# Seven products in place of eight for 37 more weight units of a streaming-encoder block

## The chip, the cores and the metric

The kernel runs on one core of a Trainium2 chip, in one launch. The metric is device time in microseconds (us) of one execution; lower is better. TensorE (PE) does matrix products into PSUM, VectorE (DVE) and ScalarE (ACT) do elementwise work, GpSimd (POOL) a little, and SyncE (SP) issues the weight transfers. Each engine runs its own instructions strictly in the order of the program, and engines wait for each other through semaphores.

## The reference

One layer of an encoder block over 256 rows of 2048 columns, all in float32:

```python
x = x + 0.5 * swiglu(rms_norm(x, ffn1_norm), ffn1_w_gate, ffn1_w_up, ffn1_w_down)
h = rms_norm(x, mix_norm)
proj = h @ w_in          # then four pooling groups and four gated-linear-attention heads
x = x + concat([y_pool, y_gla]) @ w_out
x = x + mem_cross_attention(rms_norm(x, xattn_norm), rms_norm(mem, mem_norm), w_q, w_kv, w_o)
x = x + 0.5 * swiglu(rms_norm(x, ffn2_norm), ffn2_w_gate, ffn2_w_up, ffn2_w_down)
out = rms_norm(x, final_norm)
# swiglu(h, wg, wu, wd) = (silu(h @ wg) * (h @ wu)) @ wd, with 5632 hidden columns
```

## The kernel before, in words

**Units.** The weights are streamed in units of 1 MB: a tile `raw` of 128 x 2048, three of them in flight. A float32 product is made of three products of a faster type: each factor is split into a high part (a rounded copy) and a low part (the rest), and high x high, high x low and low x high are added in PSUM. So for each unit ScalarE makes `wh` from `raw` (line 218), VectorE makes `wl = raw - wh` (line 219), and PE does 24 matmuls with 512 moving columns (`products`). `wh` and `wl` have three buffers each. The activations are held transposed and split in the same way in `xs` (what is normed from x) and `ys` (hidden rows, mixer or attention output), as 16 column groups k of 128 columns by 256 rows.

**The stream.** `Stream` (lines 34 to 90) is a list of units with other work between them: `st.op(f, n)` puts work n units later, and a unit is prepared two units ahead of its use. The order of instructions on each engine is then fixed at build time by a scheduler that plays the program through; on the chip nothing is reordered.

**Plain blocks.** `block_t` (line 293) takes eight units, four column quarters of two k-groups each, into two PSUM tiles of 128 x 2 x 512, and hands each tile to an evict function. PSUM holds four such tiles.

**Seven-product blocks.** `block_s` (line 393) takes a pair of k-groups as a 2 x 2 block product in the Strassen-Winograd form: seven products in place of eight, so 21 matmuls in place of 24. For this, sums of the weight quarters are made on VectorE in a tile `T` (lines 347 to 351, one buffer) and split into `wh` and `wl`, while the raw quarters are split into `xh` and `xl` (two buffers, 128 x 1536); the sums of activations come from `part_sums`, in a tile `xe`. Only the units 0, 2 and 4 of a block (`PAIRS`) are made in this way; the other five are plain. A block holds all four PSUM tiles: two with parts (P1, P6, P7, P5) and two with whole results. `combine` (lines 426 to 435) adds the parts up in a tile `sg`, one ScalarE copy and three VectorE adds; `join` (line 437) adds them to the whole results.

**Feed-forward.** `ffn` (line 649) goes through the hidden columns in three parts of 4, 4 and 3 groups of 512 (`FF_PARTS`). In each part come gate and up blocks by twos, an odd last column that has gate and up side by side (`wtwo`), and then the down product of the part. Gate blocks get a Silu (`ev_gate`, line 663), up blocks a product with it (`ev_up`, line 668). `turn` (line 673) transposes a finished group of hidden rows on PE into a PSUM tile `ph` and splits it into `ys`. The down product, the mixer's output product (`w_out`) and attention's (`w_o`) are written by `into_x` (line 617): two blocks, each of which adds two tiles to x (`residual`, line 595) and, where a norm follows, transposes the new x on PE and splits it into `xs` (`fold`, lines 602 to 615, with the scaled split of lines 210 and 211).

**What is seven and what is plain.** Seven-product blocks are all gate and up blocks by twos but the very first gate block of each feed-forward: 18 blocks, 54 units. Plain are those two, the odd columns, all down products, `w_out` and `w_o`. The mixer's input, q, and k/v products are made by `block_a` and `block_b` in a form of their own. The second feed-forward's last down product has a form of its own too (`down_end`).

Of the kernel before, what the change touches and what calls it, by code (L numbers as in the profile page):

```python
# [14 lines left out]
P = 128  # L15
# [77 lines left out]
def build(ctx, tc, I, out):  # L93
# [231 lines left out]
    def part_sums(act, ext, i, g):  # L325

        t = scope["pool"].tile([P, 4 * NB], F32, tag="T", name=uid("T"))
        a = t[:, :NB].rearrange("p (k s) -> p k s", k=2)
        e = t[:, NB : 2 * NB].rearrange("p (n s) -> p n s", n=4)
        nc.vector.tensor_tensor(  # L330
            out=a, in0=f32(act[:, 2 * g : 2 * g + 2, 0, :]), in1=f32(act[:, 2 * g : 2 * g + 2, 1, :]),
            op=ALU.add,
        )
        a11, a21, a12, a22 = (a[:, k, h * P : (h + 1) * P] for k in range(2) for h in range(2))
        nc.vector.tensor_tensor(out=e[:, 3], in0=a11, in1=a21, op=ALU.subtract)
        nc.vector.tensor_tensor(out=e[:, 1], in0=a22, in1=a21, op=ALU.subtract)
        nc.vector.scalar_tensor_tensor(
            out=e[:, 2], in0=e[:, 1], scalar=-1.0, in1=a11, op0=ALU.mult, op1=ALU.subtract
        )
        nc.vector.tensor_tensor(out=e[:, 0], in0=a12, in1=e[:, 2], op=ALU.add)  # L340
        split(ext[:, i, 0], ext[:, i, 1], e)
# [30 lines left out]
    def seven(banks, act, ext, i, g, first, later, weights):  # L372
# [3 lines left out]
        n4, n1, s2, s3 = ([ext[:, i, p, n] for p in range(2)] for n in range(4))  # L376
# [6 lines left out]
        order = ("P1", "P7", "P5", "P6", "P2", "P3", "P4") if first else (  # L383
            "P1", "P2", "P3", "P7", "P5", "P6", "P4")
        for n in order:
            (a, b), wh, wl = table[n]
            for j, (x, w) in enumerate(((a, wh), (a, wl), (b, wh))):
                nc.tensor.matmul(  # L388
                    banks[n], x, w, start=first and j == 0,
                    stop=not later and n in ("P1", "P5", "P6", "P7") and j == 2,  # L390
                )

    def block_s(srcs, act, ext, pairs, evict, delays=(0, 0)):

        held, n = {}, len(srcs)

        def open_banks():
            a, b, c, d = (ptile(uid("pt")) for _ in range(4))
            held["ps"] = (d, c)
            held["parts"] = (a, b)  # L400
            held["banks"] = {
                "P1": a[:, 0], "P6": a[:, 1], "P7": b[:, 0], "P5": b[:, 1],
                "P2": c[:, 0], "P4": c[:, 1], "P3": d[:, 0],
            }

        def unit_s(g):
            def fn(weights):
                if g == pairs[0]:
                    open_banks()
                seven(held["banks"], act, ext, pairs.index(g), g, g == pairs[0], g != pairs[-1],  # L410
                      weights)
            return fn

        def unit_p(g):
            def fn(wh, wl):
                wh, wl = (w.rearrange("p (k j n) -> p k j n", j=2, n=NB) for w in (wh, wl))
                for j in (1, 0):
                    for h in range(2):
                        for kk in range(2):

                            fresh = (j, h) == (0, 1) and g == min(set(range(n)) - set(pairs)) and kk == 0
                            products(held["ps"][j][:, h, :], act, 2 * g + kk, h, wh[:, kk, j],
                                     wl[:, kk, j], fresh, g == n - 1 and kk == 1)
            return fn

        def combine():
# [8 lines left out]
            nc.vector.tensor_tensor(out=e[:, 3], in0=b[:, 1], in1=e[:, 1], op=ALU.add)  # L435

        def join(j):
# [859 lines left out]
```

## Time and profile before

| what | value |
|---|---|
| median of 3 runs | 2137.7 us (2137.11 to 2137.98) |
| profiled execution | 2138.64 us |
| its span, first to last instruction | 2136.9 us |
| mean granted TensorE clock | 0.998 |
| TensorE busy | 2115.0 us, 99% |
| VectorE busy | 1425.8 us, 67% |
| ScalarE busy | 1006.0 us, 47% |

A row of the groups names line, engine, operation, the tiles written and read, the shape and the count, then the busy time and the mean length of one in ns, then the idle time of the engine just before them and what ended it. A row of the windows names a stretch and the busy time of each engine in it. A row of the chain of work that ended last has its start, its length and the line.

### The profile page before, as it was taken

How to read it: one execution, taken by the hardware profiler on the slowest of the kernel's cores; microseconds unless marked ns; L12 is line 12 of the kernel's file. 1: busy time of each engine (PE TensorE's matmuls, PEld its weight loads, DVE VectorE, ACT ScalarE, POOL GpSimd, SP SyncE). 2: the span in 40 equal slices, each digit the busy share in tenths (PEclk: the TensorE clock that was granted, in tenths of full speed). 3: DMA queues.
4: the chain of work that ended last, by engine and by line, in shares of the span. 5: the costliest groups of instructions: out<-in, count | busy, mean ns of one | idle time of the engine just before them, and what ended most of it. 6: DMA issues, size and time to landing. Idle time of an engine off the chain costs nothing.

```text
span 2136.9 us, 24071 instructions
## 1 busy us (share of the span) xinstructions
PE 2115.0 (99%) x10032; PEld 1769.1 (83%) x10032; DVE 1425.8 (67%) x1189; ACT 1006.0 (47%) x890; POOL 14.2 (1%) x41
## 2 busy tenths in 40 slices
PE   9999999999999999999999999999999999999998
PEld 7888887888888888888888888888888887888886
DVE  8786588856765576565666454567874788658744
ACT  7454354534444545455445443455443445434433
POOL 0000000000000000000000000000000000000001
PEclk9999999999999999999999999999999999999999
DMA  7556665666656655557655555666566655766663
GB/s 277 197 197 237 217 214 177 207 230 216 215 197 238 216 161 181 172 173 281 220 189 162 168 168 173 196 202 207 186 236 217 204 200 189 244 210 213 236 217 118
DMA packets 143317, 435.92 MB, mean 204 GB/s; under 512 B 9828, under 2 KB 13000, under 8 KB 142824
## 3 DMA queue, kind: packets, MB, share of 16 engines
q1 hardware_dynamic: 143176, 434.38, 60.1%
q8 instruction: 78, 1.28, 0.2%
q14 instruction: 31, 0.25, 0.0%
q10 hardware_dynamic: 32, 0.01, 0.0%
HBM read 417.58 MB, written 16.78 MB: 203 GB/s over the span
## 4 chain that ended last, share of the span: by engine, by line
PE 97%; DVE 2%; ACT 1%; issue 0%; DMA 0%; SPq 0%; DVEq 0%; ACTq 0%
PE pt L291 58%; PE pa L276 15%; PE pt L388 12%; PE pb L291 6%; PE pe L291 3%; ACT wh L218 1%; PE ph L678 1%; DVE wl L219 1%; PE pl L1071 1%; PE pv L1106 1%; PE px L608 0%; DMA x<-in_x 0%; PE px L562 0%; PE po L941 0%; DVE sg L439 0%
## 5 line engine op out<-in xcount | busy, mean ns | idle before, releaser
L219 DVE TENSOR_TENSOR wl<-raw,wh 128x2048 fp32r<-128x2048 f32 (+2 forms) x328 | 739.8, 2258 | 515.5 <-ACT wh L218 515.1
L218 ACT CAST wh<-raw 128x2048 fp32r<-128x2048 f32 (+2 forms) x329 | 618.4, 1881 | 626.3 <-PE pt L291 415.4
L291 PE MATMUL pt<-wh,xs 128*128 128x512 f32 x1952 | 620.1, 390 | 1.7 <-ACT wh L218 1.7
L291 PE MATMUL pt<-wh,ys 128*128 128x512 f32 x1728 | 534.5, 389 | 0.0
L291 PEld LDWEIGHTS pt<-wh,xs 128*128 128x128 f32 x1952 | 366.4, 188 | 78.1 <-ACT wh L218 2.5
L291 PE MATMUL pt<-wl,xs 128*128 128x512 f32 x976 | 380.4, 390 | 0.0
L291 PEld LDWEIGHTS pt<-wh,ys 128*128 128x128 f32 x1728 | 324.1, 188 | 66.8
L291 PE MATMUL pt<-wl,ys 128*128 128x512 f32 x864 | 336.3, 389 | 0.0
L276 PE MATMUL pa<-xs,wh 128*128 128x512 f32 x896 | 318.6, 399 | 2.1 <-DVE t L250 1.7
L276 PE MATMUL pa<-xs,wl 128*128 128x256 f32 x896 | 249.4, 281 | 0.0
L291 PEld LDWEIGHTS pt<-wl,xs 128*128 128x128 f32 x976 | 183.5, 188 | 37.9
L276 PEld LDWEIGHTS pa<-xs,wh 128*128 128x128 f32 x896 | 168.4, 189 | 41.6 <-issue 2.0
L291 PEld LDWEIGHTS pt<-wl,ys 128*128 128x128 f32 x864 | 162.2, 188 | 33.6
L218 ACT CAST wh<-T 128x2048 fp32r<-128x2048 f32 x54 | 103.1, 1909 | 171.1 <-DVE T L351 162.7
L219 DVE TENSOR_TENSOR wl<-T,wh 128x2048 fp32r<-128x2048 f32 x54 | 123.8, 2293 | 86.4 <-ACT wh L218 86.0
L276 PEld LDWEIGHTS pa<-xs,wl 128*128 128x128 f32 x896 | 169.9, 190 | 1.6 <-issue 0.2
L218 ACT CAST xh<-raw 128x1536 fp32r<-128x1536 f32 x54 | 80.1, 1483 | 98.6 <-DMA raw<-in_ffn_w_gate 36.6
L291 PE MATMUL pb<-wh,xs 128*128 128x512 f32 x384 | 121.7, 392 | 0.5 <-DVE ys L211 0.5
L388 PE MATMUL pt<-wh,xe 128*128 128x512 f32 x324 | 109.5, 390 | 0.8 <-DVE ys L219 0.7
L219 DVE TENSOR_TENSOR xl<-raw,xh 128x1536 fp32r<-128x1536 f32 x54 | 94.8, 1755 | 15.8 <-ACT xh L218 15.5
L291 PEld LDWEIGHTS pb<-wh,xs 128*128 128x128 f32 x384 | 72.1, 188 | 15.6 <-DVE ys L211 0.7
L388 PE MATMUL pt<-xh,xs 128*128 128x512 f32 x216 | 79.5, 391 | 0.9 <-DVE ys L219 0.9
(202 smaller groups left out, 1666.2 us busy)
## 6 DMA issues: line engine op xcount, KB each, us to landing
raw<-in_ffn_w_down SPq DMA_DIRECT2D x88, 1024.0 KB, 5.4
raw<-in_ffn_w_up SPq DMA_DIRECT2D x80, 1024.0 KB, 5.0
raw<-in_ffn_w_gate SPq DMA_DIRECT2D x77, 1024.0 KB, 5.1
raw<-in_w_in SPq DMA_DIRECT2D x32, 1024.0 KB, 5.1
raw<-in_xattn_w_kv SPq DMA_DIRECT2D x32, 1024.0 KB, 5.3
raw<-in_w_out SPq DMA_DIRECT2D x16, 1024.0 KB, 6.1
raw<-in_xattn_w_q SPq DMA_DIRECT2D x16, 1024.0 KB, 5.1
raw<-in_xattn_w_o SPq DMA_DIRECT2D x16, 1024.0 KB, 5.5
```

The costliest lines, as they stand in the source:

```text
L218: nc.scalar.copy(hi, src)
L219: nc.vector.tensor_tensor(out=lo, in0=src, in1=f32(hi), op=ALU.subtract)
L276: nc.tensor.matmul(o, w, x, start=k == 0 and i == 0, stop=last and i == 1)
L291: nc.tensor.matmul(ps, a, w, start=first and i == 0, stop=last and i == 2)
L388: nc.tensor.matmul(banks[n], x, w, start=first and j == 0, stop=not later and n in ("P1", "P5", "P6", "P7") and j == 2,)
L678: nc.tensor.transpose(v[:, i, h * P : (h + 1) * P], g[:, h, i * P : (i + 1) * P], ident)
L1071: nc.tensor.matmul(ps[:, t, :M], ys[:, 4 * h + d, a, tok], xa["K"][:, d, b, :], start=i == 0, stop=i == 11,)
L1106: nc.tensor.matmul(ps[:, d, :S], xa["V"][:, m, a, col], xa["PT"][:, m, b, :], start=i == 0, stop=i == 5,)
```

## The change

Seven products are used for 37 more units:

- both blocks of each down product that goes through `into_x`: three in the first feed-forward (12 units) and two in the second (8 units); of each block the units 0 and 1 (`Y_PAIRS`),
- `w_out` (4 units) and `w_o` (4 units), the same two units of each block, each product in a scope of its own (`out_product`),
- the odd last column of both feed-forwards (3 + 3 units),
- the first gate block of the second feed-forward (3 units).

`PAIRS` becomes (0, 1, 4), and each block gets an order of its units: `ORDER` for gate and up, `FIRST` for the second feed-forward's first gate block, `Y_ORDER` and `Y_FIRST` for the products into x. In `FIRST`, `Y_ORDER` and `Y_FIRST` two to four plain units stand before the first seven unit. In blocks into x the combined parts are added to x before the whole results are ready (`early_parts`), and the whole results then go through `residual` one by one, the second tile first. The sums are made by `Sums`: one of the four sums is written over the place in `xs` or `ys` that no product of a seven unit reads, and three are kept in a tile. The sums of `ys` in a feed-forward are made in `turn`, straight from the transposed rows in PSUM. The load and the norm of `mem` move from beside `w_out` into the units of `w_q`. The core of the diff:

```diff
-    def part_sums(act, ext, i, g):
-        t = scope["pool"].tile([P, 4 * NB], F32, tag="T", name=uid("T"))
...
+    def jtile():
+        return tmp.tile([P, NB], F32, tag="j", name=uid("j"), bufs=2)
+    class Sums:
+        def __init__(self, name, act, pairs):
+            self.name, self.act, self.pairs = name, act, pairs
+        def make(self, g, src=None):
+            act, i = self.act, self.pairs.index(g)
+            if i == 0:
+                self.tile = scope["pool"].tile(
+                    [P, len(self.pairs), 2, 3, P], F32R, tag=self.name, name=uid(self.name)
+                )
+            a, e = jtile(), jtile().rearrange("p (n s) -> p n s", n=4)
+            k = slice(2 * g, 2 * g + 2)
+            if src is None:
+                nc.vector.tensor_tensor(
+                    out=a.rearrange("p (k s) -> p k s", k=2), in0=f32(act[:, k, 0, :]),
+                    in1=f32(act[:, k, 1, :]), op=ALU.add,
+                )
+            else:
+                nc.scalar.copy(a.rearrange("p (k s) -> p k s", k=2), src)
+            b = a.rearrange("p (n s) -> p n s", n=4)
+            nc.vector.tensor_tensor(
+                out=e[:, 0:2], in0=b[:, 0:4:3], in1=b[:, 1:2].to_broadcast([P, 2, P]), op=ALU.subtract
+            )
+            nc.vector.scalar_tensor_tensor(
+                out=e[:, 2], in0=e[:, 1], scalar=-1.0, in1=b[:, 0], op0=ALU.mult, op1=ALU.subtract
+            )
+            nc.vector.tensor_tensor(out=e[:, 3], in0=b[:, 2], in1=e[:, 2], op=ALU.add)
+            split(self.tile[:, i, 0], self.tile[:, i, 1], e[:, 1:4])
+            split(act[:, 2 * g, 0, P:], act[:, 2 * g, 1, P:], e[:, 0])
+        def parts(self, g):
+            i = self.pairs.index(g)
+            s3 = [self.act[:, 2 * g, p, P:] for p in range(2)]
+            return [s3] + [[self.tile[:, i, p, n] for p in range(2)] for n in range(3)]
...
+    def block_s(srcs, act, sums, order, evict, merge=None):
+        sevens = [g for g in order if g in sums.pairs]
+        held, seen = {"banks": {}}, set()
+        def banks(*names):
+            t = ptile(uid("pt"))
+            for i, n in enumerate(names):
+                held["banks"][n] = t[:, i]
+            return t
+        def open_whole():
+            if "ps" not in held:
+                c = banks("P2", "P4")
+                held["ps"] = (banks("P3", "P0"), c)
+        def open_parts():
+            held["parts"] = (banks("P1", "P6"), banks("P7", "P5"))
...
+            if merge is not None:
+                merge(e[:, 2:4], e[:, 0:2])
         def join(j):
+            if merge is not None:
+                evict(j, held["ps"][j])
+                return
             e = held["e"][:, 0:2] if j else held["e"][:, 2:4]
             nc.vector.tensor_tensor(
                 out=e, in0=held["ps"][j], in1=e, op=ALU.add if j else ALU.subtract
             )
             evict(j, e)
 
...
+        for g in order:
+            if g in sevens:
+                st.unit(srcs[g], unit_s(g), split_seven, add_weights)
+                if g == sevens[-1]:
                     st.op(combine)
             else:
-                st.unit(src, unit_p(g))
+                st.unit(srcs[g], unit_p(g))
         for j in (1, 0):
-            st.op(lambda j=j: join(j), delays[j])
+            st.op(lambda j=j: join(j))
...
-    def residual(scale, b):
+    def residual(scale, b, last=1):
 
         def evict(j, ps):
             x = x_cols((2 * b + j) * NB, NB)
             nc.vector.scalar_tensor_tensor(
                 out=x, in0=ps, scalar=scale, in1=x, op0=ALU.mult, op1=ALU.add
             )
-            if j:
+            if j == last:
                 store_x(b)
         return evict
+    def early_parts(scale, b):
+        def merge(minus, plus):
+            for j, e, s in ((1, plus, scale), (0, minus, -scale)):
+                x = x_cols((2 * b + j) * NB, NB)
+                nc.vector.scalar_tensor_tensor(
+                    out=x, in0=e, scalar=s, in1=x, op0=ALU.mult, op1=ALU.add
+                )
+        return merge
...
-    def into_x(w, act, scale, gain=None, k0=0, nk=KT, spread_too=True, src=None):
+    def into_x(w, act, scale, gain=None, k0=0, nk=KT, spread_too=True, src=None, sums=None,
+               orders=None):
 
         for b in range(2):
             st.op(lambda b=b: fetch_x(b, src), 2)
-            block_t(wwide(w, b * 2 * NB, k0, nk), act, residual(scale, b))
+            block_s(wwide(w, b * 2 * NB, k0, nk), act, sums, orders[b], residual(scale, b, 0),
+                    early_parts(scale, b))
...
+    PAIRS, Y_PAIRS = (0, 1, 4), (0, 1)
+    FIRST = (2, 3, 5, 6, 0, 1, 4, 7)
+    ORDER = (0, 2, 1, 3, 4, 5, 6, 7)
+    Y_FIRST = (2, 3, 4, 5, 0, 6, 1, 7)
+    Y_ORDER = (2, 3, 0, 4, 1, 5, 6, 7)
+    CLEAR = 6
+    def ffn(wg, wu, wd, down, first):
         gate = {}
+        x_sums = Sums("xe", xs, PAIRS)
+        y_sums = Sums("ye", ys, Y_PAIRS)
...
+        def turn(g, k, last=False):
 
             v = four(ptile(uid("ph")))
             for i in range(4):
@@ -679,29 +728,38 @@
                         v[:, i, h * P : (h + 1) * P], g[:, h, i * P : (i + 1) * P], ident
                     )
             split(ys[:, k : k + 4, 0, :], ys[:, k : k + 4, 1, :], v)
+            if not last:
+                for g in range(k // 2, k // 2 + 2):
+                    if g in Y_PAIRS:
+                        y_sums.make(g, v[:, 2 * g - k : 2 * g - k + 2])
+        for i, g in enumerate(PAIRS):
+            st.op(lambda g=g: x_sums.make(g), 5 + i if first is None else 2 + (i == 2))
         for lo, n in FF_PARTS:
+            end = first is not None and lo + n == FF // NB
             for b in range(0, n - 1, 2):
                 n0 = (lo + b) * NB
-                if lo == b == 0:
+                up = lambda j, c: ev_gate(j, c, 0)
+                if lo == b == 0 and first is None:
                     block_t(wwide(wg, n0), xs, lambda j, ps: ev_gate(j, ps, 1))
                 else:
-                    block_s(wwide(wg, n0), xs, Ext(), PAIRS, lambda j, c: ev_gate(j, c, 0))
-                block_s(wwide(wu, n0), xs, Ext(), PAIRS, ev_up)
+                    block_s(wwide(wg, n0), xs, x_sums, first if lo == b == 0 else ORDER, up)
+                block_s(wwide(wu, n0), xs, x_sums, ORDER, ev_up)
                 held = {}
                 st.op(lambda held=held: held.update(gate))
-                wait = PAIRS[-1] + 2 if b + 2 < n - 1 else 1
+                wait = CLEAR if b + 2 < n else 1
                 for j in range(2):
-                    st.op(lambda j=j, b=b, held=held: turn(held[j], 4 * (b + j)), wait)
+                    st.op(lambda j=j, b=b, held=held, end=end: turn(held[j], 4 * (b + j), end), wait)
             if n % 2:
-                def both(j, ps):
+                def both(j, c):
                     if j:
-                        ev_up(0, ps)
+                        ev_gate(1, c, 0)
+                        gate[0] = gate[1]
                     else:
-                        ev_gate(0, ps, 1)
-                block_t(wtwo(wg, wu, (lo + n - 1) * NB), xs, both)
-                st.op(lambda n=n: turn(gate[0], 4 * (n - 1)), 1)
-            down(wd, 4 * lo, 4 * n, lo + n == FF // NB)
+                        ev_up(0, c)
+                block_s(wtwo(wu, wg, (lo + n - 1) * NB), xs, x_sums, ORDER, both)
+                st.op(lambda n=n, end=end: turn(gate[0], 4 * (n - 1), end), 1)
+            down(wd, 4 * lo, 4 * n, lo + n == FF // NB, y_sums)
...
+    def y_orders(nk, first=Y_ORDER):
+        return [[g for g in o if g < nk // 2] for o in (first, Y_ORDER)]
+    def down_first(wd, k0, nk, last, sums):
+        into_x(wd, ys, 0.5, G_MIX if last else None, k0, nk, src=None if k0 else I["x"][0],
+               sums=sums, orders=y_orders(nk))
+    ffn(I["ffn1_w_gate"][0], I["ffn1_w_up"][0], I["ffn1_w_down"][0], down_first, None)
...
+    def out_product(name, w, gain, spread_too):
+        sums = Sums("ye", ys, Y_PAIRS)
+        st.op(open_scope(name), 1)
+        for g in Y_PAIRS:
+            st.op(lambda g=g: sums.make(g), 1)
+        into_x(w, ys, 1.0, gain, spread_too=spread_too, sums=sums, orders=y_orders(KT, Y_FIRST))
+        st.op(close_scope, 1)
+    out_product("s_out", I["w_out"][0], G_X, True)
...
-    into_x(I["w_out"][0], ys, 1.0, G_X)
-    into_x(w_o, ys, 1.0, G_FFN2, spread_too=False)
+    out_product("s_o", w_o, G_FFN2, False)
+            into_x(wd, ys, 0.5, None, k0, nk, sums=sums, orders=y_orders(nk))
+    ffn(I["ffn2_w_gate"][0], I["ffn2_w_up"][0], I["ffn2_w_down"][0], down_last, FIRST)
```

In the changed program PE has 111 matmuls of 512 columns fewer, VectorE has 1498 instructions (1191 before, with those not counted as busy) and ScalarE 919 (821); the number of transfers that SP issues is the same.

More of the change, by code (lines that the diff above doesn't have):

```diff
@@ L370, in split_seven, with seven @@
         return [parts], None
-    def seven(banks, act, ext, i, g, first, later, weights):
+    def seven(banks, act, sums, g, fresh, ends, weights):
         th, tl, rh, rl = weights
@@ L375, in seven @@
         a11, a12, a22 = ([act[:, k, p, t] for p in range(2)] for k, t in ((k0, lo), (k1, lo), (k1, hi)))
-        n4, n1, s2, s3 = ([ext[:, i, p, n] for p in range(2)] for n in range(4))
+        s3, n1, s2, n4 = sums.parts(g)
         table = {
@@ L382, in seven @@
         }
-        order = ("P1", "P7", "P5", "P6", "P2", "P3", "P4") if first else (
+        order = ("P1", "P7", "P5", "P6", "P2", "P3", "P4") if "P1" in fresh else (
             "P1", "P2", "P3", "P7", "P5", "P6", "P4")
@@ L671, in ev_up @@
                 )
-        def turn(g, k):
+        def turn(g, k, last=False):
             v = four(ptile(uid("ph")))
@@ L1132, in last_gain, with down_last @@
         nc.sync.dma_start(fin["gB"], I["final_norm"].partition_broadcast(P))
-    def down_last(wd, k0, nk, last):
+    def down_last(wd, k0, nk, last, sums):
         if last:
```

74 lines of the change are left out of this document (15 added, 59 removed).

## The prediction

> **What bounds the kernel now.** I read the page first (engine shares, then the chain), then the groups of instructions for prices, then windows and the timeline of the places that the change touches.
>
> ```profile
> span 2136.9 us, 24071 instructions
> PE 2115.0 (99%) x10032; PEld 1769.1 (83%) x10032; DVE 1425.8 (67%) x1189; ACT 1006.0 (47%) x890; POOL 14.2 (1%) x41
> PE 97%; DVE 2%; ACT 1%; issue 0%; DMA 0%; SPq 0%; DVEq 0%; ACTq 0%
> ```
>
> TensorE bounds it: 99% busy, 97% of the chain. Only 21.9 us of the span are without a matmul. So work taken from PE is worth its full length, but only where the others keep up. They do by a margin that differs from stage to stage:
>
> ```profile
> 100.00:200.00 100.00, 99.26 (x455) 82.24 (x454) 79.04 (x59) 49.27 (x34) 0.00 (x0) 1.00 0.63 219
> 360.00:380.00 20.00, 19.10 (x83) 14.95 (x82) 15.69 (x12) 10.68 (x7) 0.00 (x0) 1.00 0.44 158
> 480.00:500.00 20.00, 20.00 (x90) 16.57 (x89) 10.46 (x6) 7.65 (x4) 0.00 (x0) 1.00 0.73 262
> PE pt L388 <- DVE ys L219: 1.7, 3, 0.7
> ```
>
> The columns are length, PE, PEld, DVE, ACT, POOL busy (instructions), clock, DMA share, GB/s. Where seven products are used already (first two rows), VectorE is 79% busy and PE loses a little; in a down product (third row) VectorE is 52% busy and PE loses nothing. The change carries the first kind of work into the second kind of stage.
>
> **The change part by part.** *PE.* A plain unit and a seven unit on the chain:
>
> ```profile
> 285.23 5.44 PE pt L291 x24
> 290.67 4.76 PE pt L388 x21
> ```
>
> 5.44 - 4.76 = 0.68 us less for each converted unit, and 37 units: 25.2 us. The changed program has 111 matmuls of this kind fewer, 37 x 3, so the saving on PE is certain as work. If nothing else happened the time would be 2112.5.
>
> *VectorE and ScalarE.* Prices:
>
> ```profile
> L219 DVE TENSOR_TENSOR wl<-raw,wh 128x2048 fp32r<-128x2048 f32 x320 | 732.2, 2290 | 513.5 <-ACT wh L218 513.3
> L219 DVE TENSOR_TENSOR wl<-T,wh 128x2048 fp32r<-128x2048 f32 x54 | 123.8, 2293 | 86.4 <-ACT wh L218 86.0
> L219 DVE TENSOR_TENSOR xl<-raw,xh 128x1536 fp32r<-128x1536 f32 x54 | 94.8, 1755 | 15.8 <-ACT xh L218 15.5
> L347 DVE TENSOR_TENSOR T<-raw 128x1024 f32<-128x1024 f32 x54 | 65.9, 1220 | 3.7 <-DMA raw<-in_ffn_w_up 2.2 <-DMA raw<-in_ffn_w_gate 1.2
> L439 DVE TENSOR_TENSOR sg<-pt,sg 128x1024 f32<-128x1024 f32 x36 | 43.9, 1218 | 0.4
> L351 DVE TENSOR_TENSOR T<-T,raw 128x512 f32<-128x512 f32 x54 | 37.1, 686 | 0.7
> L595 DVE SCALAR_TENSOR_TENSOR x<-pt,x 128x1024 f32<-128x1024 f32 x28 | 34.1, 1220 | 0.6
> L211 DVE SCALAR_TENSOR_TENSOR xs<-px,gains,xs 128x256 fp32r<-128x256 f32 x64 | 29.0, 479 | 2.1 <-ACT xs L210 1.5
> L219 DVE TENSOR_TENSOR ys<-ph,ys 128x1024 fp32r<-128x1024 f32 x22 | 26.2, 1218 | 2.4 <-ACT ys L218 2.4
> L432 DVE TENSOR_TENSOR sg<-pt,sg 128x1024 f32<-128x1024 f32 x18 | 22.0, 1221 | 0.3
> L435 DVE TENSOR_TENSOR sg<-pt,sg 128x512 f32<-128x512 f32 x18 | 12.3, 683 | 0.0
> L218 ACT CAST wh<-raw 128x2048 fp32r<-128x2048 f32 x320 | 611.3, 1911 | 618.6 <-PE pt L291 415.4 <-PE pa L276 76.1 <-issue 45.4
> L218 ACT CAST xh<-raw 128x1536 fp32r<-128x1536 f32 x54 | 80.1, 1483 | 98.6 <-DMA raw<-in_ffn_w_gate 36.6 <-DMA raw<-in_ffn_w_up 36.1 <-PE pt L388 25.7
> L430 ACT COPY sg<-pt 128x512 f32<-128x512 f32 x18 | 10.5, 585 | 26.7 <-PE pt L388 26.7
> ```
>
> Every converted unit adds xl and three sums on VectorE: 1.755 + 1.220 + 2 x 0.686 = 4.35 us, for 37 units 161 us. 17 blocks more are combined: 0.68 + 1.22 + 0.68 = 2.6 each, 44 us. 14 of them add the parts into x ahead of the products (2 x 1.22 each, 34 us); the other three join like the old ones (7 us). The 14 sums of ys take some 1.9 us each in narrow subtractions, 27 us. Together 273 us: VectorE goes from 1426 to about 1700, 80% of the span. ScalarE gets 37 x 1.48 + 17 x 0.585 and narrow copies, about 85 us: 51%. As averages both fit. In a down block of 8 units VectorE now has 2 x 6.65 + 6 x 2.29 + 2.6 + 4 x 1.22 = 34.5 us beside 42.2 us of PE, 82%; gate and up blocks stay near 90%. So the bulk is hidden, and what counts are the places where PE waits for the end of a VectorE queue.
>
> *End of w_o, start of the second feed-forward.* Before:
>
> ```profile
> 1394.95 23.81 PE pt L291 x105
> 1418.76 1.75 PE px L608 x16
> 1420.51 19.54 PE pt L291 x86
> 1412.06 2.51 DVE L595 SCALAR_TENSOR_TENSOR x<-pt,x 128x1024 f32<-128x1024 f32 x2
> 1421.08 2.29 DVE L219 TENSOR_TENSOR wl<-raw,wh 128x2048 fp32r<-128x2048 f32 x1 [0.45 <-ACT wh L218]
> 1423.29 0.48 DVE L211 SCALAR_TENSOR_TENSOR xs<-px,gains,xs 128x256 fp32r<-128x256 f32 x1
> 1430.47 0.87 DVE L211 SCALAR_TENSOR_TENSOR xs<-px,gains,xs 128x256 fp32r<-128x256 f32 x2
> ```
>
> The last w_o block ends one unit before 1418.76, at 1413.3. Its residuals run at once, the first L211 starts 10 us after the end, and columns 8 to 11 of xs are wanted only by the fifth unit, 4 x 5.44 + 1.75 = 23.5 us after the end. The new first gate block takes its units as 2, 3, 5, 6, 0, 1, 4, 7: the third wants columns 10 and 11, 2 x 5.44 + 1.75 = 12.6 us after the end (14 for column 11). In the changed order VectorE holds, from the block's end to the fourth L211 of those columns: wl of four units (9.2), residuals 2 x 1.22, seven L211 (3.4), two xl (3.5), a T (2.6), two and a half sets of sums with their splits (5.3), and the norm's small ones (1.0): 27 us. Neighbours overlap a little (2.21 between the starts at 1421.08 and 1423.29, for a 2.29): about 25. Less 14 that leaves 8 to 12 us; I take 10. It cannot be under 0, and the upper end is 27 - 12.6 = 14.
>
> *End of the first feed-forward, start of the mixer.* Before:
>
> ```profile
> 699.83 25.84 PE pt L291 x114
> 725.67 5.64 PE pa L276 x32
> 731.32 1.75 PE px L608 x16
> 733.06 5.45 PE pa L276 x31
> 724.42 2.51 DVE L595 SCALAR_TENSOR_TENSOR x<-pt,x 128x1024 f32<-128x1024 f32 x2
> ```
>
> The last residual ends 1.3 us after the block (726.93 against 725.67). After, this block has six units, and its second seven unit is the last but one. Combine, two merges and two residuals, with wl of three units between them, then follow each other on VectorE: 0.68 + 1.22 + 2.29 + 0.68 + 1.22 + 2.29 + 1.22 + 1.22 + 2.29 + 1.22 = 14.3 us from the end of the seven unit, of which the last unit covers 5.44 less a little. The second residual ends 9 to 10 us after the block. PE's transposes of it stand in PE's queue one unit (5.64) behind the block's end and hold every product behind them: 3.4 to 4.4 us there, and up to 1 more where the third unit waits for L211. 3 to 5.5 us; I take 4.5.
>
> *The clock.* What a long wait costs beyond itself:
>
> ```profile
> 906.00:912.00 6.00, 3.34 (x24) 2.53 (x23) 4.89 (x9) 4.61 (x5) 0.00 (x0) 1.00 0.37 143
> 912.00:914.00 2.00, 2.00 (x9) 1.71 (x9) 2.00 (x5) 0.14 (x1) 0.00 (x0) 0.68 0.89 205
> 914.00:916.00 2.00, 2.00 (x7) 1.71 (x7) 1.91 (x5) 1.63 (x3) 0.00 (x0) 0.50 0.77 315
> 916.00:918.00 2.00, 2.00 (x12) 1.68 (x12) 1.53 (x3) 1.81 (x3) 0.00 (x0) 0.96 0.01 4
> ```
>
> After a stretch in which PE was busy 3.34 of 6 us the granted clock was 0.68, 0.50 and 0.96 in three windows of 2 us: 0.64 + 1.00 + 0.08 = 1.7 us lost. I add 2 us for the wait of 10, nothing for the shorter ones; from 0 to 1.7 at each of six.
>
> The Trainium skill ("TensorE: Matmul & The Clock Gate", section "What's actually happening") says that after an idle window of some 3.4 us the array falls to half clock until it has been busy as long; the rows above agree in kind. By it each wait of that length would pay again, and the sum would be that of the clock rival below.
>
> *Turning the hidden rows, with sums of ys.* Now turn's PSUM tile goes on being read by two ScalarE copies after its split. At the next boundary those copies stand behind a join and two Silu, and the second join behind two wl (2.29), a T sum (1.22) and the split of ys (1.22), while the next block waits for the join's and turn's PSUM slots. By such a queue PE waits some 3 us, before 0.9 (the 360 to 380 row). At four places 2 us more each, 0.7 to 4: 8; below it 0, since a slot may be free by luck.
>
> *Odd columns and block boundaries.* The odd column's last two units and the block before it are now both seven-blocks that hand over four PSUM tiles, at four places, and gate to up, down to gate at eight: 0 to 2.5 each, by the one or two 1.22 adds in front of the release. I take 0.5: 6 us.
>
> *At nothing:* the sums of the two output products and the memory's load and norm moved into w_q. The plain units there leave VectorE half idle (as in the 480 to 500 row); uncovered, 3 us. In the first gate block two seven units stand side by side, and their one T buffer passes through 1.22 + 2 x 0.69 + 1.91 + 2.29 = 6.8 us for 4.76 of PE: 0 to 2 us, at nothing because VectorE gets ahead in the wait before them. No DMA is added; SP issues the same transfers, the memory's two later, ahead of work that needs them three w_q blocks on.
>
> Sum: -25.2 + 10 + 4.5 + 2 + 8 + 6 = +5.3. Profiled execution 2138.64 (span 2136.9 and 1.7 around it), 0.9 above the median 2137.7; carried to the median: 2143.
>
> **The rivals.** *Only the two boundaries stall* (faster): the turn and column waits vanish if VectorE runs ahead in the blocks before them; two of three windows above show it with a fifth to spare. -25.2 + 16.5 = -8.7: 2129. It decides from 14 us of small waits downwards; against it speaks that PE waits there already. *All is hidden*: 2112.5. It needs the queue of 25 us to pass in 14. *VectorE saturates*: one 1.22 us add in front of each of the 14 new residual blocks costs 17 us more, 2160. *The clock falls behind every wait*: 1.7 us at six places in place of my 2 gives 8 more, 2151; one place in this trace shows it, the waits of under 1 us do not. *The change does nothing to PE*: excluded by the 111.
>
> **How the numbers follow.** Under 0.2%, 4.3 us, nothing can be told from no change. Chances: forecast 0.45 (2134 to 2151: 0.29 above 2142, 0.16 within), two boundaries 0.27 (0.25 faster, 0.02 within), all hidden 0.10, saturated 0.12, clock 0.06. So faster 0.35, same 0.18, slower 0.47. The range reaches to both sides without the fully hidden case and the worst of saturation: 2120 to 2160; the forecast's own is 2134 to 2151.
>
> **What would show it.** In the profile after: PE busy near 2090 and idle near 50; windows at the start of the second feed-forward with some 10 us lost and a clock under 1.0 behind it, waits there for L211's xs; 4 to 5 us lost after the first feed-forward; waits of seven's pt for VectorE's splits at the turns, 2 to 3 us each. The prediction is wrong if the first gate block runs without a gap, or if the 20 us windows of down products lose PE time in their middle.

## The result and the profile after

| | before | changed |
|---|---|---|
| median | 2137.8 us (2137.1 to 2140.7, 4 runs) | 2155.7 us (2151.9 to 2158.4, 4 runs) |
| ratio, 95% interval | 1 | 1.0080 (1.0062 to 1.0098) |
| profiled execution, span | 2138.64, 2136.9 us | 2151.87, 2150.1 us |

The change made the kernel slower by 0.8%. The direction is the one forecast, and the time lies inside the range of 2120 to 2160. It lies outside the forecast's own 2134 to 2151, and the size was forecast too small: +5.3 for the profiled execution, which showed +13.2 (its span 2150.1 against 2136.9); the median shows 17.9. The page after, first lines and chain:

```profile
span 2150.1 us, 24306 instructions
PE 2102.5 (98%) x9921; PEld 1749.6 (81%) x9921; DVE 1668.5 (78%) x1496; ACT 1078.8 (50%) x988; POOL 15.2 (1%) x41
PE 80%; DVE 8%; ACT 4%; DMA 3%; issue 2%; SPq 0%; DVEq 0%; ACTq 0%
```

TensorE has its 111 matmuls fewer (10032 to 9921), but its share of the chain fell from 97% to 80%, VectorE and ScalarE now have 12%, and weight loads 3% (before, 0%). VectorE grew by 243 us, ScalarE by 73 (273 and 85 were forecast). PE's idle time went from 21.9 to 47.6 us. PE's busy time fell by 12.5 us and not by 25.2: when the clock is low, or when a matmul waits for less than its own recorded length, the loss stands inside the busy time (for the clock see the windows at 370 us in the last section: PE counts as busy 2.00 of 2 us at a clock of 0.50).

Where it went is seen best by cutting the span at the first and the last product into x of each stage (starts and ends of these matmuls in PE's timeline; the stage of w_out ends at the first product of the first v block). Lengths in us; the last column is the work that the stage saves, at 0.68 per converted unit. Each length is that of one execution. In this kernel and three of those below, with the same code up to there, the first hidden part took 185.0 to 188.2, so a difference of a microsecond or two in one stage can be chance:

| stage | before | changed | difference | saved products |
|---|---|---|---|---|
| start, first hidden part | 181.3 | 185.0 | +3.7 | 0 |
| its down product | 89.0 | 86.2 | -2.8 | 2.7 |
| second hidden part | 170.2 | 173.5 | +3.3 | 0 |
| down | 89.0 | 86.3 | -2.7 | 2.7 |
| third part with odd column | 128.1 | 130.1 | +2.0 | 2.0 |
| down | 68.1 | 66.5 | -1.6 | 2.7 |
| mixer | 211.5 | 213.6 | +2.1 | 0 |
| w_out, q, first k | 202.9 | 202.0 | -0.9 | 2.7 |
| v, k and attention | 181.4 | 181.4 | 0 | 0 |
| w_o | 91.9 | 92.9 | +1.0 | 2.7 |
| second feed-forward, first part | 172.1 | 183.9 | +11.8 | 2.0 |
| down | 89.0 | 86.3 | -2.7 | 2.7 |
| second part | 169.5 | 171.8 | +2.3 | 0 |
| down | 89.0 | 86.3 | -2.7 | 2.7 |
| third part with odd column | 128.1 | 128.8 | +0.7 | 2.0 |
| last down product | 66.3 | 66.4 | 0 | 0 |

The four long down products give all that was hoped for. The stages of hidden rows ahead of a seven down product give back 2.3 to 4.0 each, and one stage gives back 11.8. Three of these stages hold a fall of the clock, to half for a few us and with some 1.7 us lost, that the kernel before does not have there (at 369.86, 629.27 and 1434.82 us; see the last section). Windows after, with the columns of the prediction (its second and third row are the first two stretches before; for the last stretch the second fence has the kernel before):

```profile
360.00:380.00 20.00, 18.62 (x73) 14.36 (x72) 16.05 (x13) 9.55 (x6) 0.00 (x0) 0.91 0.58 207
480.00:500.00 20.00, 20.00 (x90) 16.56 (x89) 18.38 (x13) 8.50 (x5) 0.00 (x0) 1.00 0.84 304
1420.00:1440.00 20.00, 14.16 (x63) 10.78 (x61) 19.90 (x34) 15.20 (x26) 0.00 (x0) 0.91 0.71 255
```

```profile
1420.00:1440.00 20.00, 20.00 (x92) 16.61 (x91) 17.16 (x30) 11.48 (x15) 0.00 (x0) 1.00 0.59 196
```

In a down product (second row) VectorE went from 52% to 92% and PE still loses nothing. At the start of the second feed-forward (third row) PE is idle 5.8 of 20 us while VectorE is busy 19.9, and the clock falls behind it. The timeline of VectorE there:

```profile
1417.74 2.35 DVE L639 SCALAR_TENSOR_TENSOR x<-pt,x 128x1024 f32<-128x1024 f32 x2
...
1427.21 0.47 DVE L211 SCALAR_TENSOR_TENSOR xs<-px,gains,xs 128x256 fp32r<-128x256 f32 x1
1427.59 1.22 DVE L372 TENSOR_TENSOR T<-raw 128x1024 f32<-128x1024 f32 x1
...
1431.92 1.76 DVE L219 TENSOR_TENSOR xl<-raw,xh 128x1536 fp32r<-128x1536 f32 x1
...
1437.56 2.28 DVE L219 TENSOR_TENSOR wl<-T,wh 128x2048 fp32r<-128x2048 f32 x1
1439.77 0.87 DVE L211 SCALAR_TENSOR_TENSOR xs<-px,gains,xs 128x256 fp32r<-128x256 f32 x2
```

The w_o block ends at 1417.5, and the pair of L211 for which PE waits last starts at 1439.77, 22.3 us later, behind a sum of weights, two xl and a wl of units that PE wants only afterwards. PE came to that unit at 1430.0, 12.5 us after the end. Its waits name it (the last row is of the kernel before):

```profile
PE pt L291 <- ACT wh L218: 5.8, 7, 0.8
PE pt L413 <- ACT j L350: 5.1, 3, 1.7
PE pt L291 <- ACT xs L210: 5.1, 1, 5.1
PE pt L413 <- ACT wh L218: 3.9, 6, 1.0
PE pa L276 <- DVE xs L211: 3.2, 2, 2.8
PE pt L291 <- DVE wl L219: 2.3, 2, 1.6
```

```profile
PE pt L291 <- ACT wh L218: 1.7, 2, 0.8
```

The third row is the start of the second feed-forward, ended by ScalarE's half of the scaled split (line 210); another 1.1 us went to VectorE's half. The second row are the turns of the hidden rows, the fifth is led by the start of the mixer, and the sixth are two waits in w_o.

The waits for `wh`, first and fourth row, are the largest group: 9.7 us, 1.7 before. The longer ones all stand in hidden parts. The chain of the changed kernel shows a weight load ahead of the one at 369 us:

```profile
354.88 1.41 DVE sg L717 x2
356.29 2.21 DVE wl L219
...
358.52 5.03 DMA raw<-in_ffn_w_gate
...
363.65 0.06 ACT xh L218
...
365.03 3.71 ACT wh L218 x2
```

Products with the gate and a `wl` on VectorE come first, then the load of a weight unit that has to wait for a buffer, then two casts, and PE goes on at 368.78. Twelve such loads, 62 us, are on the chain after, and none before. The forecast has no term for this path. No run gives `raw` more buffers, so what it costs stays open. A load on the chain is not by itself a loss: the run without VectorE's sums of ys below has 3% there too, and is as fast as the kernel before.

### The profile page after: what moved, and what is told of

Its sections match the earlier page's. It is cut to its first block, busy times and chain, and to the rows that moved or that the text cites. A ratio compares the mean times of both kernels' runs of the same rounds, so it can differ in the third digit from the quotient of the medians.

```text
span 2150.1 us, 24306 instructions
## 1 busy us (share of the span) xinstructions
PE 2102.5 (98%) x9921; PEld 1749.6 (81%) x9921; DVE 1668.5 (78%) x1496; ACT 1078.8 (50%) x988; POOL 15.2 (1%) x41
## 4 chain that ended last, share of the span: by engine, by line
PE 80%; DVE 8%; ACT 4%; DMA 3%; issue 2%; SPq 0%; DVEq 0%; ACTq 0%
PE pt L291 37%; PE pt L413 16%; PE pa L276 14%; PE pb L291 6%; DVE wl L219 4%; ACT wh L218 3%; PE pe L291 3%; DMA raw<-in_ffn_w_gate 2%; DMA raw<-in_ffn_w_up 1%; DVE xl L219 1%; DVE sg L483 1%; PE ph L727 1%; PE pl L1139 1%; PE pv L1174 1%; DVE T L372 1%
## 5 line engine op out<-in xcount | busy, mean ns | idle before, releaser
L219 DVE TENSOR_TENSOR wl<-raw,wh 128x2048 fp32r<-128x2048 f32 (+2 forms) x291 | 654.2, 2252 | 262.2 <-ACT wh L218 261.8
L218 ACT CAST wh<-raw 128x2048 fp32r<-128x2048 f32 (+2 forms) x292 | 546.5, 1876 | 318.2 <-PE pt L291 91.7
L291 PE MATMUL pt<-wh,xs 128*128 128x512 f32 x1808 | 582.5, 392 | 11.9 <-ACT wh L218 5.8
L291 PE MATMUL pt<-wh,ys 128*128 128x512 f32 x1280 | 402.1, 389 | 0.0
L218 ACT CAST wh<-T 128x2048 fp32r<-128x2048 f32 x91 | 173.9, 1911 | 246.8 <-DVE T L376 238.5
L219 DVE TENSOR_TENSOR wl<-T,wh 128x2048 fp32r<-128x2048 f32 x91 | 208.5, 2291 | 95.2 <-ACT wh L218 94.4
L291 PEld LDWEIGHTS pt<-wh,ys 128*128 128x128 f32 x1280 | 240.2, 188 | 50.1 <-ACT wh L218 0.4
L291 PE MATMUL pt<-wl,ys 128*128 128x512 f32 x640 | 249.2, 390 | 2.3 <-DVE wl L219 2.3
L291 PEld LDWEIGHTS pt<-wl,xs 128*128 128x128 f32 x904 | 170.3, 188 | 35.3 <-DVE wl L219 0.4
L219 DVE TENSOR_TENSOR xl<-raw,xh 128x1536 fp32r<-128x1536 f32 x91 | 159.7, 1755 | 27.8 <-ACT xh L218 27.8
L372 DVE TENSOR_TENSOR T<-raw 128x1024 f32<-128x1024 f32 x91 | 111.0, 1220 | 4.2 <-DMA raw<-in_ffn_w_down 2.8
L413 PE MATMUL pt<-wh,xs 128*128 128x512 f32 x252 | 99.8, 397 | 10.5 <-ACT j L350 5.1
```

The costliest lines, as they stand in the source:

```text
L218: nc.scalar.copy(hi, src)
L219: nc.vector.tensor_tensor(out=lo, in0=src, in1=f32(hi), op=ALU.subtract)
L291: nc.tensor.matmul(ps, a, w, start=first and i == 0, stop=last and i == 2)
L372: nc.vector.tensor_tensor(out=v[:, 0:2], in0=w[:, 1:3], in1=w[:, 0:1].to_broadcast([P, 2, NB]), op=ALU.add)
L413: nc.tensor.matmul(banks[n], x, w, start=n in fresh and j == 0, stop=n in ends and j == 2)
```

## The experiments

Each of them is the changed kernel with one edit, or the first experiment with one more; the last two join several. Ratios are against the kernel before, with 95% intervals.

### The second feed-forward's first gate block plain again

```diff
-    ffn(I["ffn2_w_gate"][0], ..., down_last, FIRST)
+    ffn(I["ffn2_w_gate"][0], ..., down_last, None, True)   # block_t for the first gate block
```

> The changed kernel with the second feed-forward's first gate block plain again (8 plain units), the rest as changed. Theory (the early need of columns 10 and 11 behind a long VectorE queue is what costs 6 us of idle and a clock drop there): the stage from the end of w_o to the first down product of the second feed-forward goes from 183.9 us to about 175 (172.1 before, and some 3 us of turn waits), the kernel to about 2147. Rival (VectorE is saturated in the feed-forward, and what is not lost here is lost a block later): the stage stays over 180 and the kernel over 2152.

Measured: 2146.8 us, ratio 1.0045 (1.0030 to 1.0060); the stage is 173.2 us. In its window PE is busy again without a gap:

```profile
1420.00:1440.00 20.00, 20.00 (x98) 16.75 (x98) 18.59 (x36) 15.89 (x27) 0.00 (x0) 1.00 0.77 266
```

The theory holds: three units that save 2.0 us cost 12.7 (10.7, of which 1.7 is a fall of the clock, and the 2.0 given back). The sums of xs are made one or two units later in this version as well. The loss did not move to a later block: the next hidden part took 173.8 against 171.8, with a fall that the changed kernel does not have there, the third 128.1 against 128.8.

### The same plain block in the changed order

```diff
-    block_t(wwide(wg, n0), xs, ...)
+    block_t(wwide(wg, n0), xs, ..., order=FIRST)   # 2, 3, 5, 6, 0, 1, 4, 7
```

The sums of xs now stand in xs before units 0, 1 and 4 are multiplied, so this block's values for them are not the reference's; the work is the same.

> As the run with the plain first gate block in the second feed-forward, but its plain units taken in the changed order 2, 3, 5, 6, 0, 1, 4, 7, so that columns 10 and 11 are wanted as early as in the changed kernel while the seven units' sums and splits are gone from the front of VectorE's queue. If the early need alone makes the wait, the stage comes to 180 us or more (183.9 changed, 173.2 with the plain block in natural order). If it takes the seven units' VectorE work in front of the fold's, it stays within 2 us of 173.2, the kernel within 3 us of 2146.8.

Measured: 2149.4 us, 1.0049 (1.0034 to 1.0064); stage 178.8. Neither answer is right alone. The early need costs 5.6 us even with plain units (PE 16.48 of 20 us there, and one fall of the clock); the seven units' work in the queue adds 183.9 + 2.0 - 178.8 = 7.1. This is read from one execution of each; the ratios of this kernel and of the first experiment do not tell the two apart.

```profile
1420.00:1440.00 20.00, 16.48 (x74) 13.07 (x73) 17.03 (x36) 13.14 (x26) 0.00 (x0) 0.91 0.71 255
```

### Sums of ys from ys and not out of PSUM

```diff
-                        y_sums.make(g, v[:, 2 * g - k : 2 * g - k + 2])
+                        y_sums.make(g)
```

> The changed kernel, with turn's sums of ys made from the split rows in ys by a VectorE add of 128x512 (0.69 us, ten more) in place of ScalarE copies out of PSUM, so that turn's PSUM tile is free after its split. Theory A (the PSUM tile held by the copies is what costs the hidden stages 3.7, 3.2 and 2.4 us): each of these stages loses 1 us or less against before, the kernel comes to about 2147. Theory B (the VectorE queue at that boundary is what costs): the stages get longer by 0.7 to 1.4 us each, the kernel about 2159.

Measured: 2154.9 us, 1.0082 (1.0067 to 1.0097): no change, and neither theory's time. The second part of the first feed-forward shrinks to 171.2, by no more than a fall of the clock that it no longer holds and half a microsecond; that of the second goes from 171.8 to 172.4, with a fall more. The down products behind them grow from 86.3 to 87.9, and the two together stay about where they were (259.1 against 259.7 changed and 259.2 before, in the first feed-forward). The free PSUM tile gave nothing in sum.

### Sums of ys at the start of the down product

```diff
+            if not end:
+                for g in Y_PAIRS:
+                    st.op(lambda g=g: y_sums.make(g), 0)
             down(wd, 4 * lo, 4 * n, lo + n == FF // NB, y_sums)
```

(and none in `turn`).

> The changed kernel, with the sums of ys taken out of turn and made from ys at the start of the down product. Theory A and B of the boundary (sums in turn are the cost, by PSUM or by VectorE): the hidden stages of parts 1 and 2 come to within 1 us of before (181.3, 170.2 and 169.4), the down products lose at most 1 us each of their 2.7, the kernel about 2147. Rival C (the cost is the new order of the pairs, with the seven units 0, 1 and 4): the hidden stages keep their 3 us, the kernel stays at 2154 to 2158.

Measured: 2156.0 us, 1.0088 (1.0071 to 1.0105). The second part came to 170.9 in the first feed-forward (170.2 before), to 172.5 in the second (169.5; 1.7 of it a fall of the clock), and the down products behind them to 87.9; the kernel did not gain. Its time is the one that rival C gave, and not that of A and B; the second parts are nearer to A and B. The next run parts them. The same work costs about the same at the one side of the boundary as at the other.

### All down products plain

```diff
-    into_x(wd, ys, 0.5, ..., sums=sums, orders=y_orders(nk))
+    into_x(wd, ys, 0.5, ..., sums=sums)          # block_t; no sums in turn
```

> The changed kernel with all down products plain and no sums of ys in the feed-forwards (odd columns, first gate block, w_out and w_o as changed). Theory A or B: the hidden stages return to their lengths of before, which saves 9 to 12 us, the down products give back 12.5, and the kernel stays within 3 us of 2155.7. Rival C (order of the pairs): the stages keep their loss and the kernel goes to 2165 or more.

Measured: 2151.5 us, 1.0072 (1.0049 to 1.0094), 4 us under the changed kernel by the medians, though the two intervals overlap. The second parts are 170.3 and 169.5, their lengths of before, with the new pairs in them; the third parts 127.8 (128.1 before, with 2.0 of products less). So rival C falls for these stages, and in the profiled executions the down products' seven units cost 4.2 us more than they save (the sums of the stages are 2141.0 and 2136.8). The changed kernel has three falls of the clock more in these executions, 5.1 us; without them its seven units would about pay.

### VectorE's part of the sums of ys left out

On the first experiment, whose time is 2146.8:

```diff
                 nc.scalar.copy(a..., src)
+                nc.scalar.copy(self.tile[:, i, 0], b[:, 1:4])
+                nc.scalar.copy(self.tile[:, i, 1], b[:, 1:4])
+                nc.scalar.copy(act[:, 2 * g, 0, P:], b[:, 0])
+                return
```

> The run with the plain first gate block, with the VectorE part of turn's sums of ys left out: ScalarE copies the rows out of turn's PSUM tile as before and writes copies where the sums would stand, so the down products multiply rows that are no sums, with the same work on PE. If VectorE's work at that boundary is the cost (theory B), the part 2 stages fall from 173.5 to 171 or less with the down products still at 86.3, kernel about 2139. If the PSUM tile that the copies hold is the cost (theory A), the stages stay at 173 or more, kernel 2145 to 2149.

Measured: 2138.0 us, 1.0003 (0.9994 to 1.0013). Some 50 narrow VectorE instructions, 14 us of busy time (1651.8 to 1637.7), are worth 8.8 us of the kernel. Two falls of the clock fewer are part of it (3 against 5, below). The wait for turn's copies, 5.4 us in the first experiment, is gone from the list, though the copies still read the same PSUM tile. In the first experiment:

```profile
PE pt L413 <- ACT j L350: 5.4, 3, 2.0
```

The stages of the second parts fell to 172.1 and 170.8, the first part of the second feed-forward to 171.7. Theory B (VectorE's work at the boundary) holds in the kernel's time, and one of the two second parts meets its number; the other holds a fall of the clock. One reading joins both theories, and was not tried: the copies go into a tile `j` with two buffers, so the second pair of them can only run when VectorE is done with the first.

### The sums spread over the second up block

On the first experiment:

```diff
+                if b == 0 and not end:
+                    for g in Y_PAIRS:
+                        st.op(lambda g=g: y_sums.make(g), 11 + 2 * g if n == 4 else 7 + g)
```

(and none in `turn`).

> The run with the plain first gate block, and the sums of ys made one by one from ys in the middle of the second up block (parts of four groups), away from the block boundaries. If the boundary is what makes them dear, the two stages of part 2 (173.5 with 86.3 for the down product) become 171 and 86.3, the first parts gain 2 each too, kernel about 2140. If VectorE has no room anywhere (the same work costs the same wherever it stands), hidden stage and down product together stay at 259 to 260, kernel 2145 to 2149.

Measured: 2143.9 us, 1.0023 (1.0012 to 1.0035), 3 us better, and with the last experiment (1.0020) the best seen with seven down products and right sums. Hidden part and down product together are 260.3 in the first feed-forward and 258.7 in the second. Neither answer is met: the time lies between the 2140 of the one and the 2145 of the other, and the two together shrank nowhere by more than a fall of the clock. Its profiled execution has 2 falls, that of the first experiment 5.

### Pairs 0, 2 and 4 again

On the first experiment, `PAIRS = (0, 2, 4)`, `ORDER = (0, 1, 2, 3, 4, 5, 6, 7)`.

> The run with the plain first gate block, and the pairs back to 0, 2 and 4 in natural order in gate, up and odd blocks. The first hidden stage was 183.3 us even without sums of ys (181.3 before). If the new order of the pairs costs these 2 us, this stage falls by about 2 against 185 to 187.6, the others do not change, kernel 2143 to 2145. If it is the new way to make the sums of xs, or clock drops that fall here by chance, the stage stays over 184 and the kernel at 2145 to 2149.

Measured: 2145.1 us, 1.0036 (1.0024 to 1.0048); first stage 188.8 with one fall of the clock. The median fits the first answer, the stage does not; the order of the pairs is not shown to cost anything, and the 2 us of the first part stay open.

### Combined parts earlier in the second block

On the first experiment, the second block of each product into x takes 2, 0, 3, 1, 4, 5, 6, 7.

> The run with the plain first gate block, with the second block of each product into x in the order 2, 0, 3, 1, 4, 5, 6, 7, so that the combined parts are in x one or two units earlier. Theory (the late residual holds the fold's transposes): the mixer's stage goes from 213.6 back to 211.5, and w_o to the next stage gains a little; kernel about 2144. Rival (the residual is not what the mixer waits for): it stays at 213 or more; and the seven units may now wait for PSUM tiles of the block before, which would make the down products longer than 86.3.

Measured: 2146.0 us, 1.0039 (1.0026 to 1.0052); the mixer's stage is 216.1, longer (it holds two falls of the clock, one in the changed kernel), the four long down products are 86.9 to 87.0, and the short one 68.6 (66.5 changed). My theory of the mixer's wait falls. In w_o the earlier combine did gain: its stage went from 92.9 to 91.0, and of two waits for `wl` there, 1.59 and 0.70 us, one of 1.24 is left. What PE waits for is seen in the chain of the changed kernel:

```profile
727.65 11.17 PE pa L276 x63
738.82 0.02 issue
738.85 1.91 ACT wh L218
740.76 0.03 issue
740.78 2.29 DVE wl L219
743.07 0.41 DVE xs L211
```

The residual was late as forecast (the second one ends at 735.66, 8 us after the block), but the transposes were ordered behind two units and did not wait. L211 stands in VectorE's queue behind the wl of a unit, whose wh ScalarE can cast only when PE has finished two more units and freed a buffer: 1.91 + 2.29 + 0.41 from 738.82 on. In the experiment the chain has the same three, behind the squares of the new x on ScalarE, and nothing of the residuals is in it.

### Only odd columns and w_out

> Of the change, only the odd columns and the mixer's output product are left as seven (with the new pairs and orders); down products, w_o and the first gate block are plain and no sums of ys are made in the feed-forwards. 10 units keep 6.8 us of saved products. If VectorE has room outside the places found so far, the kernel comes to 2131 to 2133, below the kernel before. If each converted unit costs about what it saves in the stage where it stands (odd columns gained 0.3 of 2.0 so far, w_out 0.1 to 1.1 of 2.7), it comes to 2135 to 2139.

Measured: 2141.5 us, 1.0018 (1.0008 to 1.0028), a little slower than before and worse than both answers: w_out with q took 204.8 us and one fall of the clock, and the first hidden part 184.0 (181.3 before). The fall does not explain the time, since the kernel before has one too, in the mixer. Even these ten units do not pay.

### The best pieces together

> Plain first gate block, plain w_o, sums of ys spread over the second up block; the down products, odd columns and w_out seven. By the stages measured so far: 2143.9 for the spread sums less 1.0 for w_o, 2143; under 2138 only if the stage after w_o gains as well.

Measured: 2143.1 us, 1.0020 (1.0010 to 1.0030), as summed up. No version beat the kernel before.

## Why the prediction was right, and where it was too small

The direction and the kind of place were right: with the seven units out of the first gate block and VectorE's sums of ys left out, the kernel is back at 1.0003. That the range of 2120 to 2160 holds the result is owed to its upper end, which was set by a rival; the forecast's own range misses it. Of the signs that it named, PE's idle time came out (47.6 us for some 50), PE's busy time did not (2102.5 for 2090).

*The saved work*, 25.2 us, is there: 2.7 in each of four down products. In the run at 1.0003, 34 units are still seven and save 23 us, so about as much is still lost there in places whose causes were not all taken apart.

*VectorE is not saturated as a whole.* At 92% in a down product PE loses nothing. That rival's mechanism (an add in front of each release) did not show in the four long down products, though its time of 2160 is nearer than mine. In w_out, w_o and the short down product PE did wait for a late `wl`: 0.86, 1.59 and 0.70, and 0.78 us, places for which the forecast had 0.5 each at most.

*Start of the second feed-forward*: forecast 10 and 2 for the clock; measured 12.7 with the clock in it. The queue was as listed, 22.3 us and not 25, since VectorE came in a little ahead (one of the four wl ended with the block, at 1417.8); both causes, need and queue, showed in the stage, 5.6 and 7.1.

*Start of the mixer*: forecast 4.5; measured 2.1, and 1.1 that its down product kept. The step "the transposes hold every product" failed: the residual was late, but the wait is for L211 behind a wl whose buffer PE frees. That the size came near is luck.

*Turns*: this term was mis-sized and its cause in part wrong. Forecast 8 at four places, by the PSUM tile. Against the run with plain down products the six hidden parts lost 1.7, 3.2, 2.3, 3.1, 2.3 and 1.0, together 13.6 us. Two falls of the clock are 3.4 of that, and the last 1.0 stands in a part where both kernels run the same work. Freeing the tile gained nothing, leaving VectorE's narrow work out gained 8.8. The waits of seven's pt were forecast for VectorE's splits; three of 1.7 us each were put down to ScalarE's copies, one of 1.5 to a split.

*Odd columns and boundaries*: forecast 6; measured 11: 1.7 in each third part (127.8 where 126.1 was due), 3.7 in w_o, 1.8 in w_out, 2.0 in the first part. An earlier combine gave w_o 1.9 back; what causes the others was not taken apart, and the path by way of a late weight load is one that the forecast did not have.

*The clock*: "nothing for the shorter ones" is a step that failed. I put the rival of falls behind every wait at 0.06. The row that I took for one long wait, 906 to 912 us of the kernel before, holds two, of 1.01 and 1.65 us. The profiled execution after has three falls more than before, 5.1 us where 2 were forecast, and they stand inside the stage losses above; the other three executions, 3.1 to 6.5 us longer than it, have a mean granted clock of 0.993 to 0.995 against its 0.996.

The sum of the losses: 12.7 + 3.2 + 13.6 + 11 = 40.5 where 30.5 was forecast, less some 2 that two terms share in the first part of the second feed-forward.

## What to carry to other kernels

Work that another engine can carry on average is paid for at the places where one queue must drain before the bottleneck goes on: sum the queue in order from the block's end to the instruction that is wanted, and compare it with the work the bottleneck has until then; that sum came out within 3 us here. Small instructions at such a place cost much of their length, 8.8 us of 14 here, falls of the clock included. And each new wait on TensorE may cost another 1.7 us of low clock, so many short waits must be priced with that chance.

## What was unexpected of the hardware

The clock fell after waits shorter than the prediction reckoned with. Changed kernel, 366 to 374 us, and the same place of the kernel before:

```profile
366.00:368.00 2.00, 1.43 (x6) 0.53 (x4) 1.95 (x2) 2.00 (x2) 0.00 (x0) 1.00 0.86 352
368.00:370.00 2.00, 1.19 (x4) 0.78 (x5) 2.00 (x2) 0.73 (x1) 0.00 (x0) 0.96 0.00 0
370.00:372.00 2.00, 2.00 (x6) 1.55 (x5) 2.00 (x2) 0.00 (x0) 0.00 (x0) 0.50 0.04 8
372.00:374.00 2.00, 2.00 (x8) 1.56 (x7) 1.93 (x3) 0.00 (x0) 0.00 (x0) 0.68 0.66 147
```

```profile
366.00:368.00 2.00, 1.13 (x4) 0.39 (x4) 2.00 (x2) 1.25 (x1) 0.00 (x0) 1.00 0.02 8
368.00:370.00 2.00, 2.00 (x10) 1.62 (x11) 2.00 (x2) 0.00 (x0) 0.00 (x0) 1.00 0.03 8
```

Waits of 0.6 and 0.8 us, 1.4 of 4 us, were followed by a clock of 0.96, 0.50 and 0.68, a loss of 0.04 x 2 + 0.50 x 2 + 0.32 x 2 = 1.7 us; a wait of 0.9 before was not. Nor does the length alone decide. At 142 to 146 us the changed kernel was idle 1.5 us and kept its clock; there the first experiment, with the same code up to that place, was idle 2.2 us and lost it:

```profile
142.00:144.00 2.00, 1.70 (x8) 1.09 (x6) 2.00 (x3) 0.00 (x0) 0.00 (x0) 1.00 0.58 113
144.00:146.00 2.00, 0.79 (x3) 0.67 (x4) 2.00 (x3) 0.58 (x1) 0.00 (x0) 1.00 0.97 387
```

```profile
144.00:146.00 2.00, 0.14 (x1) 0.00 (x0) 2.00 (x3) 0.59 (x1) 0.00 (x0) 1.00 0.91 254
146.00:148.00 2.00, 1.63 (x5) 1.29 (x6) 2.00 (x4) 0.52 (x1) 0.00 (x0) 0.68 0.66 266
148.00:150.00 2.00, 2.00 (x6) 1.61 (x5) 1.59 (x6) 1.93 (x4) 0.00 (x0) 0.50 0.00 0
```

Windows cut at the edges of the stretch of low clock at 370 us and just ahead of it show its length, 3.41 us at half the clock, with 3.41 - 2.03 = 1.38 us of waiting in the 3.41 us before it:

```profile
366.45:369.86 3.41, 2.03 (x7) 1.16 (x7) 3.36 (x3) 2.28 (x2) 0.00 (x0) 1.00 0.37 151
369.86:373.27 3.41, 3.41 (x9) 2.65 (x8) 3.38 (x3) 0.00 (x0) 0.00 (x0) 0.50 0.26 40
```

The four low stretches of the changed kernel ahead of the tail begin at 369.86, 629.27, 915.99 and 1434.82. The distances between them are 76, 84 and 152 times 3.413 us, so within this execution they keep to a beat. Counted back on that beat, an edge lies at 144.58, inside the wait of 1.5 us that ended at 145.21 and cost nothing: 0.88 us of it fell to one side and 0.63 to the other. In the first experiment the stretch of 3.41 us ahead of the fall at 146.74 holds the whole wait of 2.2 us.

The Trainium skill ("TensorE: Matmul & The Clock Gate", section "What's actually happening") says that activity is counted in windows of some 3.4 us that run freely and do not start anew with the kernel. The runs agree with that: the low stretches keep to a beat of 3.41 us, and whether 1.4 to 2.2 us of waiting cost a fall differs from place to place and from execution to execution. The rule in the same page's section "HAM oscillation — how this bites in real kernels", no idle gaps above some 3.4 us, is not enough by these runs: here no single wait ahead of the falls at 370 and 146 was longer than 2.2 us.

In the profiled executions of the eleven experiments 1 to 6 falls of about 1.7 us each were counted ahead of the tail, 4 in that of the changed kernel and 1 in that of the kernel before.
